# Second product of both squared-ReLU MLPs by Strassen's algorithm in a two-layer trunk

## The chip, the cores and the metric

One core of a Trainium2 chip. Its engines are TensorE (PE, matrix products out of SBUF into PSUM), VectorE (DVE), ScalarE (ACT), GpSimd (POOL) and SyncE (SP, which starts the DMA transfers). Each has its own list of instructions and executes it in that order; semaphores make one wait for another. The time is the device time of one launch in microseconds (us), and lower is better.

## The reference, cut to what matters

A hidden state h of 1040 tokens (16 learned ones ahead of 1024) by 1024 features goes through two layers. Layer 0 has a mixer of recurrent channels, layer 1 a chunked state-space mixer (SSD); each is followed by the same kind of MLP, and both with a residual.

```
SEQ, N_META, D_MODEL, D_FF, DEPTH = 1024, 16, 1024, 4 * 1024, 2

def sq_relu_mlp(h, w_up, w_down):
    return jnp.square(jax.nn.relu(h @ w_up)) @ w_down

h = jnp.concatenate([meta, x], axis=1)
for layer in range(DEPTH):
    hn = rmsnorm(h, norm_mix[layer])
    mix = even_mixer(hn, ...) if layer % 2 == 0 else ssd_mixer(hn, ...)
    h = h + mix
    h = h + sq_relu_mlp(rmsnorm(h, norm_mlp[layer]), mlp_w_up[layer], mlp_w_down[layer])
h = rmsnorm(h, norm_final)
return h[:, N_META:]
```

The first product of an MLP makes 4096 hidden features from 1024, the second makes 1024 from 4096. Everything is float32. After the mixer of layer 1 the 16 learned tokens are not needed any more, so its MLP works on 1024 tokens.

## The kernel before

The state lies in SBUF with features on the 128 partitions: 8 feature tiles (KT) by tokens. Tokens come in three tiles: 400, 384 and 256 in the MLP of layer 0 (TT), 384, 384 and 256 in that of layer 1 (TL). PE takes float32 data here in a rounded form (fp32r), so each operand is split into a rounded part "hi" and the rest "lo", and one product of float32 matrices is three matmuls: hi by hi, hi by lo and lo by hi (mm3, L160 to L164). A matmul multiplies a 128 by 128 block of weights with as many columns as there are tokens in the tile. Weights come from HBM in halves of 512 columns (wraw); ACT rounds them (L156) and DVE, for some of them POOL, subtracts (L157).

An MLP has 32 tiles of 128 hidden features, taken in 16 blocks of two. do_up makes the hidden tiles of a block: for each of three token tiles and both feature tiles one up_unit of 24 matmuls (8 feature tiles by three) into one PSUM tile. DVE then applies the relu and the factor of the norm (L356), POOL squares (L357), ACT rounds (L358) and DVE subtracts (L359). do_down is the second product: for each token tile and each of the 8 output tiles n, 6 matmuls (two hidden tiles by three) into one PSUM tile, which DVE adds to the state (L400: "h<-h,mm"). So a block has 6 x 24 = 144 matmuls in its first product and 3 x 8 x 6 = 144 in its second.

The main loop emits the first product of block b + 1 ahead of the second product of block b. The last pass does the second products of the last two blocks together, 12 matmuls for each PSUM tile, and beside each added output tile it squares and sums for the next norm and splits the state where the next stage wants it so (L263, L286 to L288; after layer 1 the final norm). The weights of the first product have two buffers of each of two tags (w, u), those of the second two of tag d. PSUM has 8 banks of 512 float32 columns: four buffers "mm" for products and four "sm" for sums.

The order in each engine's list is made when the program is built, by a scheduler that starts from the order in which the code emits and moves an instruction forward where it reckons that its operands and buffers are ready; `shifted` gives some functions an earlier or later place. No table of numbers sets it by hand.

## Time and profile before

| | |
|---|---|
| median of 3 runs | 2831.54 us (2829.19 to 2836.15) |
| the profiled execution | 2833.13 us, its span in the trace 2831.4 us, granted TensorE clock 0.986 on the average |
| MLP of layer 0 | its first evictions (L400) at 435.7 us, its last pass from about 1070 to 1118 us |
| MLP of layer 1 | from about 2100 us, last pass from about 2771 to 2819 us, last eviction at 2819.5 us |
| instructions on PE and DVE | 17625 matmuls, 4043 DVE instructions |

The profile is one execution, taken by the hardware profiler. A busy PE means that a matmul is in flight; matmuls overlap, so how fast they follow each other is read from the distance between their starts in the timeline. The granted clock is TensorE's, 1.00 being the full 2.4 GHz. "idle before" is time in which an engine waited for the releaser named. Names after the arrow are the tiles that an instruction reads, the ones ahead of it what it writes.

### The profile page before, as it was taken

To read this page: it belongs to the slowest core of one execution; us is meant where nothing else is said; L and a number is where in the kernel's file an instruction comes from. 1 tells how busy PE (TensorE), PEld (TensorE's weight loads), DVE (VectorE), ACT (ScalarE), POOL (GpSimd) and SP (SyncE) were. 2 spreads that over 40 slices of the span, in tenths; PEclk is the share of its full clock that TensorE was granted. 3 is DMA by queue.
4 is the path that set the end of the run, shared out by engine and by line. 5 is a ranking of instruction groups with operands and counts; after the bars stand their busy time and mean duration, and the time that the engine had idled before them with its cause. 6 is when DMAs were issued, how large, how long until landed. Compare 5 with 4: busy or idle time off the path is not lost.

```text
span 2831.4 us, 45178 instructions
## 1 busy us (share of the span) xinstructions
PE 2740.4 (97%) x17625; PEld 2676.8 (95%) x17625; DVE 1832.7 (65%) x4043; ACT 927.5 (33%) x1953; POOL 626.5 (22%) x765
## 2 busy tenths in 40 slices
PE   7998999999999999999999999999899999999998
PEld 7887999999999999899999999998889999999998
DVE  9887465555555556776876767778884555555555
ACT  4556241112111113444443444435551112121113
POOL 2212121101010113243332333324441111010112
PEclk9989999999999999999999999999999999999999
DMA  4432320101111110121221212213321101011111
GB/s 163 110 77 57 120 68 31 60 31 60 38 53 51 40 60 18 51 79 53 73 74 44 80 51 70 77 50 110 95 68 37 60 31 60 30 60 42 49 49 60
DMA packets 117909, 176.37 MB, mean 62 GB/s; under 512 B 13376, under 2 KB 47936, under 8 KB 117568
## 3 DMA queue, kind: packets, MB, share of 16 engines
q1 hardware_dynamic: 117408, 173.34, 19.8%
q8 instruction: 138, 2.26, 0.3%
q14 instruction: 75, 0.61, 0.1%
q10 hardware_dynamic: 288, 0.15, 0.0%
HBM read 158.34 MB, written 8.72 MB: 59 GB/s over the span
## 4 chain that ended last, share of the span: by engine, by line
PE 77%; DVE 15%; ACT 2%; issue 2%; DMA 2%; POOL 1%; SPq 0%; DVEq 0%; POOLq 0%; ACTq 0%
PE mm L163 24%; PE mm L162 24%; PE mm L164 23%; DVE xbc L1094 3%; DMA csb<-csd 1%; PE mm L1204 1%; DVE lo L288 1%; PE sm L1208 1%; PE mm L1201 1%; PE sm L1167 1%; PE sm L250 1%; DVE wlo L157 1%; DVE zs L1230 1%; PE sm L233 0%; DVE xbc L1096 0%
## 5 line engine op out<-in xcount | busy, mean ns | idle before, releaser
L162 PE MATMUL mm<-hi,whi 128*128 128x256 f32 (+2 forms) x2400 | 787.5, 328 | 16.1 <-ACT whi L156 8.5
L164 PE MATMUL mm<-hi,wlo 128*128 128x256 f32 (+2 forms) x2400 | 772.2, 322 | 3.1 <-POOL wlo L157 3.1
L163 PE MATMUL mm<-lo,whi 128*128 128x256 f32 (+2 forms) x2400 | 773.9, 323 | 1.2 <-POOL lo L280 0.6
L400 DVE TENSOR_TENSOR h<-h,mm 128x384 f32<-128x384 f32 (+1 forms) x720 | 368.8, 512 | 301.6 <-PE mm L164 299.6
L162 PEld LDWEIGHTS mm<-hi,whi 128*128 128x128 f32 x2400 | 456.6, 190 | 22.0 <-ACT whi L156 9.7
L164 PEld LDWEIGHTS mm<-hi,wlo 128*128 128x128 f32 x2400 | 456.3, 190 | 4.2 <-POOL wlo L157 3.8
L163 PE MATMUL mm<-hl,dhi 128*128 128x384 f32 (+2 forms) x1440 | 459.5, 319 | 0.0
L164 PE MATMUL mm<-hh,dlo 128*128 128x384 f32 (+2 forms) x1440 | 459.4, 319 | 0.0
L163 PEld LDWEIGHTS mm<-lo,whi 128*128 128x128 f32 x2400 | 455.5, 190 | 4.2 <-POOL lo L280 0.9
L162 PE MATMUL mm<-hh,dhi 128*128 128x384 f32 (+2 forms) x1440 | 459.3, 319 | 0.1
L357 POOL TENSOR_TENSOR s<-s 128x384 f32<-128x384 f32 (+2 forms) x192 | 162.7, 848 | 1187.8 <-DVE s L356 1086.3
L156 ACT CAST dhi<-wraw 128x512 fp32r<-128x512 f32 x120 | 68.9, 620 | 651.0 <-PE mm L163 574.8
L162 PEld LDWEIGHTS mm<-hh,dhi 128*128 128x128 f32 x1440 | 271.9, 189 | 0.3 <-DVE h L400 0.3
L164 PEld LDWEIGHTS mm<-hh,dlo 128*128 128x128 f32 x1440 | 272.0, 189 | 0.0
L163 PEld LDWEIGHTS mm<-hl,dhi 128*128 128x128 f32 x1440 | 271.9, 189 | 0.0
L163 PE MATMUL mm<-lo,uhi 128*128 128x384 f32 (+2 forms) x768 | 245.3, 319 | 0.0
L164 PE MATMUL mm<-hi,ulo 128*128 128x384 f32 (+2 forms) x768 | 245.0, 319 | 0.0
L162 PE MATMUL mm<-hi,uhi 128*128 128x384 f32 (+2 forms) x768 | 244.9, 319 | 0.0
L1094 DVE SCALAR_TENSOR_TENSOR xbc<-s,cols,xbc 128x400 f32<-128x400 f32 (+2 forms) x288 | 205.4, 713 | 25.6 <-ACT xbc L1092 23.5
L358 ACT CAST hh<-s 128x384 fp32r<-128x384 f32 (+2 forms) x192 | 92.3, 481 | 393.1 <-POOL s L357 393.1
L359 DVE TENSOR_TENSOR hl<-s,hh 128x384 fp32r<-128x384 f32 (+2 forms) x192 | 99.5, 518 | 147.5 <-ACT hh L358 145.2
L356 DVE SCALAR_TENSOR_TENSOR s<-mm,rb 128x384 f32<-128x384 f32 (+2 forms) x192 | 98.9, 515 | 146.4 <-PE mm L164 143.2
(367 smaller groups left out, 4400.0 us busy)
## 6 DMA issues: line engine op xcount, KB each, us to landing
wraw<-in_mlp_up SPq DMA_DIRECT2D x128, 256.0 KB
wraw<-in_mlp_down SPq DMA_DIRECT2D x128, 256.0 KB
wraw<-in_ssd_in SPq DMA_DIRECT2D x120, 256.0 KB
csb<-csd SPq DMA_DIRECT2D x64, 256.0 KB
sa<-ecd SPq DMA_DIRECT2D x128, 64.0 KB
wraw<-in_ssd_out SPq DMA_DIRECT2D x32, 256.0 KB
wraw<-in_ev_in SPq DMA_DIRECT2D x24, 256.0 KB
wraw<-in_ev_out SPq DMA_DIRECT2D x18, 256.0 KB
```

The lines of the kernel that those rows point to most:

```text
L156: nc.scalar.copy(hi[:, s], raw)
L157: e.tensor_tensor(out=lo[:, s], in0=raw, in1=hi[:, s].bitcast(F32), op=ALU.subtract)
L162: nc.tensor.matmul(pt, lhsT=whi, rhs=xhi, start=first, stop=False)
L163: nc.tensor.matmul(pt, lhsT=whi, rhs=xlo, start=False, stop=False)
L164: nc.tensor.matmul(pt, lhsT=wlo, rhs=xhi, start=False, stop=last)
L250: self.nc.tensor.matmul(st[:, o:o + l], lhsT=y[:l, i:i + 1].broadcast_to([l, P]), rhs=self.ident[:l, :l], start=True, stop=True)
L356: nc.vector.scalar_tensor_tensor(out=r, in0=pt[:, :w], scalar=0.0, in1=rbs[i], op0=ALU.max, op1=ALU.mult)
L357: nc.gpsimd.tensor_tensor(out=sq, in0=r, in1=r, op=ALU.mult)
L358: nc.scalar.copy(hh, sq)
L359: nc.vector.tensor_tensor(out=hl, in0=sq, in1=hh.bitcast(F32), op=ALU.subtract)
L400: nc.vector.tensor_tensor(out=hs, in0=hs, in1=pt[:, :w], op=ALU.add)
L1094: v.scalar_tensor_tensor(out=ot, in0=raw[:, k:k + w], scalar=cw(k), in1=ot, op0=ALU.mult, op1=ALU.add)
```

## The change

In 14 of the 16 blocks of each MLP the second product is done by the Strassen-Winograd scheme. The block's weights (two hidden tiles by 1024 outputs) and its hidden squares (two hidden tiles by all tokens) are each cut in four quarters: hidden tile 0 or 1; lower or upper half of the outputs (4 tiles each); lower or upper half of the tokens, 520 each in layer 0 and 512 each in layer 1. Seven products of a combination of weight quarters with a combination of hidden quarters take the place of eight. Four of the seven go straight into a quarter of the state ("2", "5", "3", "4"), and three into sums in SBUF ("1", "6", "7": acc, 4 output tiles by half of the tokens each) that are kept over all 14 blocks and spread over the state once, by 14 additions of two output tiles by half of the tokens (combine). For that, one quarter of the state is subtracted from another at the start. The 15th block is done in eight quarter products ("c11" to "c22"), while combine runs; the last pass now holds one block, four output tiles at a time.

The combinations are made by POOL into two buffers, ca for weights and cb for the hidden layer. Each operand of a product, a piece, is rounded by ACT and its low part subtracted by POOL for weights (sw) and by DVE for the hidden layer (sx); hi and lo lie together in one of six buffers "pc". Weights of the second product come in four quarters of 512 columns (draw, six buffers). The pieces of a product are emitted two products ahead of it. Hidden squares are no more split when they are made: ACT squares into one tile, and POOL's square and DVE's subtraction (L357, L359) are gone. A product has one piece of weights (128 by 512) and one of the hidden layer (128 by 520 or 512) and four output tiles: in layer 0 four PSUM pairs of two banks, each one output tile with 2 x 260 tokens, 6 matmuls a pair and 24 a product; in layer 1 two pairs, each two output tiles with 512 tokens, again 6 matmuls a pair, 12 a product. An eviction takes a whole pair (L502 of the changed kernel). In the MLP's blocks PSUM holds three such pairs (pd) and two single banks (ps) for everything else, and for the last pass it goes back to four and four.

The first product's units now go hidden tile by hidden tile with the three token tiles inside, and one unit is emitted after each product.

```diff
+        self.H = cp.tile([P, KT, NTOK], F32, name="h")
+        self.h = [self.H[:, :, o:o + w] for o, w in TT]
...
+    def psum(self, wide):
+        if self.pstack:
+            self.pstack.close()
+        self.pstack = st = ExitStack()
+        self.npsum += 1
+        pool = lambda name, bufs: st.enter_context(self.tc.tile_pool(name=f"{name}{self.npsum}", bufs=bufs, space=PSUM))
+        self.pd = pool("pd", 3) if wide else None
+        self.ps = pool("ps", 2 if wide else 4)
+        self.pss = None if wide else pool("pss", 4)
...
+        if tag == "pc":
+            hi, lo = (self.piece(pool)[:, :1024] for _ in range(2))
...
-    def up_unit(self, tls, ws, i, f, pool, tag, rbs):
-        r, sq = self.scr("s0", w), self.scr("s1", w)
-        hh, hl = (pool.tile([P, w], F32R, name=f"{q}{tag}{i}{f}", bufs=1) for q in ("hh", "hl"))
+        r = self.scr("s0", w)
         nc.vector.scalar_tensor_tensor(out=r, in0=pt[:, :w], scalar=0.0, in1=rbs[i], op0=ALU.max, op1=ALU.mult)
-        nc.gpsimd.tensor_tensor(out=sq, in0=r, in1=r, op=ALU.mult)
-        nc.scalar.copy(hh, sq)
-        nc.vector.tensor_tensor(out=hl, in0=sq, in1=hh.bitcast(F32), op=ALU.subtract)
+        nc.scalar.activation(out=dst[:, o - t0:o - t0 + w].bitcast(F32), in_=r, func=AF.Square)
         self.tick()
-        return hh, hl
+    def piece(self, mp):
+        return mp.tile([P, self.pcw], F32R, name="pc", bufs=6)
+    def split2(self, mp, x, e):
+        nc = self.nc
+        w = x.shape[-1]
+        t = self.piece(mp)
+        hi, lo = t[:, :w], t[:, w:2 * w]
+        nc.scalar.copy(hi, x)
+        e.tensor_tensor(out=lo, in0=x, in1=hi.bitcast(F32), op=ALU.subtract)
+        return hi, lo
...
+        NB = 16
+        t0, hw, subs = (0, 520, ((0, 260), (260, 260))) if layer == 0 else (META, 512, ((0, 512),))
+        halves = slice(t0, t0 + hw), slice(t0 + hw, t0 + 2 * hw)
+        rbs = {} if rbs is None else rbs
+        W, sq = dict(enumerate(ahead)), {}
+        if early:
+            sq[0] = [early[f] for f in range(2)]
+        def hidden(b):
+            if b not in sq:
+                q = ep if ep and b % 2 == 0 else mp
+                sq[b] = [q.tile([P, 2 * hw], F32R, name=f"sq{f}" if ep else f"sq{b % 2}{f}", bufs=1) for f in range(2)]
+            return sq[b]
...
+        def ups(b):
+            hid = hidden(b)
+            for f in range(2):
+                for i in range(3):
+                    if not (early and b == 0 and i == 0):
+                        self.up_unit(tls, [W[2 * b], W[2 * b + 1]], i, f, ep if ep and i == 0 else mp, hid[f], t0, rbs)
+                        yield
+                n = 2 * b + f + 2
+                if n < 32 and n not in W:
+                    W[n] = self.load_w(up[n])
...
+                    r = mp.tile([P, 512], F32, name="draw", bufs=6)
+                    nc.sync.dma_start(r, down[2 * b + f][:, q * 512:q * 512 + 512])
...
+        sw = lambda x: self.split2(mp, x, pool)
+        sx = lambda x: self.split2(mp, x, v)
+        def seven(b):
+            (w11, w12, w21, w22), (b11, b12, b21, b22) = quarters(b)
+            ca = mp.tile([P, 512], F32, name="ca", bufs=1)
+            cb = mp.tile([P, hw], F32, name="cb", bufs=1)
+            def comb(a0, a1, aop, x0, x1):
+                pool.tensor_tensor(out=ca, in0=a0, in1=a1, op=aop)
+                if x0 is not None:
+                    pool.tensor_tensor(out=cb, in0=x0, in1=x1, op=ALU.subtract)
+            yield "1", [(sw(w11), sx(b11))]
+            yield "2", [(sw(w12), sx(b21))]
+            comb(w21, w22, ALU.add, b12, b11)
+            yield "5", [(sw(ca), sx(cb))]
+            comb(ca, w11, ALU.subtract, b22, cb)
+            yield "6", [(sw(ca), sx(cb))]
+            comb(w12, ca, ALU.subtract, None, None)
+            yield "3", [(sw(ca), sx(b22))]
+            pool.tensor_tensor(out=cb, in0=b21, in1=cb, op=ALU.subtract)
+            yield "4", [(sw(w22), sx(cb))]
+            comb(w11, w21, ALU.subtract, b22, b12)
+            yield "7", [(sw(ca), sx(cb))]
...
+        def eight(b):
+            (w11, w12, w21, w22), (b11, b12, b21, b22) = quarters(b)
+            a = sw(w11), sw(w12)
+            x = sx(b11), sx(b21)
+            yield "c11", list(zip(a, x))
...
+        acc = {k: mp.tile([P, 4, hw], F32, name=f"acc{k}", bufs=1) for k in "167"}
+        H = lambda r, c: self.H[:, 4 * r:4 * r + 4, halves[c]]
+        dest = {"1": acc["1"], "6": acc["6"], "7": acc["7"], "2": H(0, 0), "5": H(1, 1), "3": H(0, 1), "4": H(1, 0),
+                "c11": H(0, 0), "c12": H(0, 1), "c21": H(1, 0), "c22": H(1, 1)}
+        step = 2 if len(subs) == 1 else 1
+        def product(key, pairs, copy):
+            for m in range(0, 4, step):
+                pt = self.pd.tile([P, 1024], F32, name="pd")
+                p2 = pt.rearrange("p (a b) -> p a b", a=2)
+                for q in range(2):
+                    n, (o, w) = (m + q, subs[0]) if step == 2 else (m, subs[q])
+                    ns = slice(n * P, n * P + P)
+                    for j, ((ah, al), (xh, xl)) in enumerate(pairs):
+                        self.mm3(p2[:, q, :w], ah[:, ns], al[:, ns], xh[:, o:o + w], xl[:, o:o + w], j == 0, j == len(pairs) - 1)
+                d = dest[key][:, m:m + step]
+                if step == 1:
+                    d = d.rearrange("p a (s w) -> p (a s) w", s=2)
+                src = p2[:, :, :subs[0][1]]
+                if copy and key in acc:
+                    nc.scalar.copy(d, src)
+                else:
+                    v.tensor_tensor(out=d, in0=d, in1=src, op=ALU.add)
+        def combine():
+            add = lambda a, b, n: v.tensor_tensor(out=a[:, n:n + 2], in0=a[:, n:n + 2], in1=b[:, n:n + 2], op=ALU.add)
+            a1, a6, a7 = (acc[k] for k in "167")
+            for x, y in (H(0, 0), a1), (a6, a1), (H(0, 1), H(1, 1)), (a7, a6), (H(0, 1), a6), (H(1, 0), a7), (H(1, 1), a7):
+                for n in (0, 2):
+                    add(x, y, n)
+                yield
...
+        self.psum(True)
+        for n in range(0, 4, 2):
+            d = H(0, 1)[:, n:n + 2]
+            v.tensor_tensor(out=d, in0=d, in1=H(1, 1)[:, n:n + 2], op=ALU.subtract)
+        items = (it for b in range(NB - 1) for it in (seven(b) if b < NB - 2 else eight(b)))
+        queue = deque()
+        fetch = lambda: queue.append(next(items))
...
-        for b in range(NB - 2):
-            nh = do_up(b + 1)
-            wd = down_w(b)
-            for i in range(3):
-                do_down([(wd, hid)], i)
-            hid = nh
+        for b in range(NB - 2):
+            u = ups(b + 1)
+            for j in range(7):
+                if j == 3:
+                    rows(b + 1)
+                last = b == NB - 3 and j > 4
+                if not last:
+                    fetch()
+                elif j == 6:
+                    fetch()
+                product(*queue.popleft(), b == 0)
+                next(u, None)
...
+        u = ups(NB - 1)
+        com = combine()
+        for j in range(4):
+            if j < 3:
+                fetch()
             else:
+                wd = [self.load_w(down[2 * NB - 2], mp, "pc")]
+            product(*queue.popleft(), False)
+            for _ in range(2):
+                next(u, None)
+                next(com, None)
...
+        wd.append(self.load_w(down[2 * NB - 1], mp, "pc"))
+        self.psum(False)
...
+        for i, (o, w) in enumerate(tls):
+            off = o - TT[i][0]
+            hs = lambda n: self.h[i][:, n, off:off + w]
+            pts = {}
+            for n in range(KT):
+                for f, m in ((f, m) for f in range(2) for m in (range(n, n + 4) if n % 4 == 0 else ())):
+                    if f == 0:
+                        pts[m] = self.mm()
+                    ms = slice(m * P, (m + 1) * P)
+                    h, q = (z[:, o - t0:o - t0 + w] for z in hid[f])
+                    self.mm3(pts[m][:, :w], wd[f][0][:, ms], wd[f][1][:, ms], h, q, f == 0, f == 1)
+                v.tensor_tensor(out=hs(n), in0=hs(n), in1=pts[n][:, :w], op=ALU.add)
```

Line numbers after the change are those of the changed kernel: its mm3 has L179 to L181, the weights' subtraction L174, a hidden piece's subtraction L386, the relu eviction L372, the product's eviction L502, the last pass's eviction L583.

PE in layer 0, where a block's last unit of the first product ends (mm_5972, third token tile) and the second product begins (mm_6025), before:

```order
L162 MATMUL mm_5972<-hi2_80,whi_5797 128x256
L163 MATMUL mm_5972<-lo2_83,whi_5797 128x256
L164 MATMUL mm_5972<-hi2_80,wlo_5798 128x256
L162 MATMUL mm_6025<-hh000_5404,dhi_6005 128x400
L163 MATMUL mm_6025<-hl000_5405,dhi_6005 128x400
L164 MATMUL mm_6025<-hh000_5404,dlo_6006 128x400
L162 MATMUL mm_6025<-hh001_5437,dhi_6015 128x400
```

After the change, PE at the joint of two blocks of layer 0: the last pair of product "7" (pd_5496) and the first of product "1" of the next block (pd_5522); each pd is a PSUM pair:

```order
L179 MATMUL pd_5496<-pc_5335,pc_5332 128x260
L180 MATMUL pd_5496<-pc_5335,pc_5332 128x260
L181 MATMUL pd_5496<-pc_5335,pc_5332 128x260
L179 MATMUL pd_5522<-pc_5403,pc_5400 128x260
L180 MATMUL pd_5522<-pc_5403,pc_5400 128x260
L181 MATMUL pd_5522<-pc_5403,pc_5400 128x260
L179 MATMUL pd_5522<-pc_5403,pc_5400 128x260
```

The end of the third pair of the same product and its fourth pair (pd_5538, pd_5546), a little further in the same list:

```order
L180 MATMUL pd_5538<-pc_5403,pc_5400 128x260
L181 MATMUL pd_5538<-pc_5403,pc_5400 128x260
L179 MATMUL mm_5556<-hi0_76,whi_5292 128x400
L180 MATMUL mm_5556<-lo0_79,whi_5292 128x400
L181 MATMUL mm_5556<-hi0_76,wlo_5293 128x400
L179 MATMUL mm_5556<-hi0_76,whi_5292 128x400
L180 MATMUL mm_5556<-lo0_79,whi_5292 128x400
L179 MATMUL pd_5546<-pc_5403,pc_5400 128x260
L180 MATMUL pd_5546<-pc_5403,pc_5400 128x260
L181 MATMUL pd_5546<-pc_5403,pc_5400 128x260
```

Before, 144 matmuls of the first product are followed by 144 of the second, each PSUM tile a single bank. After, no unit of the first product stands between products "7" and "1", so eight pairs follow each other, broken only by five matmuls of the next unit (mm_5556) ahead of the eighth pair.

DVE in one block of the middle of layer 0, before. h_75, h_76, h_77 are the state's three token tiles, s a relu'd tile, dlo and wlo low parts of weights:

```order
L356 SCALAR_TENSOR_TENSOR s_7254<-mm,rb_4024 128x256
L359 TENSOR_TENSOR hl_7257<-s_7255,hh_7256 128x256
L356 SCALAR_TENSOR_TENSOR s_7287<-mm,rb_4024 128x256
L400 TENSOR_TENSOR h_75<-h_75,mm 128x400
L359 TENSOR_TENSOR hl_7290<-s_7288,hh_7289 128x256
L400 TENSOR_TENSOR h_75<-h_75,mm 128x400 x7
L400 TENSOR_TENSOR h_76<-h_76,mm 128x384 x8
L400 TENSOR_TENSOR h_77<-h_77,mm 128x256 x8
L157 TENSOR_TENSOR dlo<-wraw,dhi 128x512 x4
```

DVE at the joint of two blocks of layer 0 after the change. acc_3842 is the sum "7", acc_3840 the sum "1", pc<-cb the low part of a hidden piece, wlo that of a weight of the first product:

```order
L372 SCALAR_TENSOR_TENSOR s_7833<-mm,rb_3979 128x256
L174 TENSOR_TENSOR wlo<-wraw,whi 128x512
L502 TENSOR_TENSOR acc_3842<-acc_3842,pd 128x520 x4
L174 TENSOR_TENSOR wlo<-wraw,whi 128x512
L386 TENSOR_TENSOR pc<-cb,pc 128x520
L502 TENSOR_TENSOR acc_3840<-acc_3840,pd 128x520 x4
L386 TENSOR_TENSOR pc<-cb,pc 128x520
L372 SCALAR_TENSOR_TENSOR s_7951<-mm,rb_3898 128x400
L502 TENSOR_TENSOR h<-h,pd 128x520 x4
L386 TENSOR_TENSOR pc<-sq_7451,pc 128x520
L372 SCALAR_TENSOR_TENSOR s_8019<-mm,rb_3947 128x384
L502 TENSOR_TENSOR h<-h,pd 128x520 x4
```

Before, the 24 evictions of a block stand in one row, with the four weight subtractions of the next block behind them. After, they come in rows of four, one for each product, and between them stand the relu evictions, the weight subtractions and the subtractions of pieces for products to come.

## Rows read from the trace of the kernel before

**Rows 1.** The page's first part: engine, busy us (share of the span) xinstructions.

```profile
span 2831.4 us, 45178 instructions
...
PE 2740.4 (97%) x17625; PEld 2676.8 (95%) x17625; DVE 1832.7 (65%) x4043; ACT 927.5 (33%) x1953; POOL 626.5 (22%) x765
```

**Rows 2.** Windows in the MLPs: start:end, us, busy by engine (instructions), PEclk, DMA, GB/s.

```profile
700.00:800.00 100.00, 100.00 (x648) 100.00 (x647) 53.13 (x96) 16.68 (x31) 11.87 (x15) 1.00 0.14 43
1070.00:1118.00 48.00, 47.93 (x307) 47.38 (x306) 29.70 (x69) 17.51 (x37) 13.07 (x13) 1.00 0.05 15
1110.00:1140.00 30.00, 27.46 (x165) 25.93 (x164) 29.90 (x77) 16.05 (x37) 12.84 (x19) 0.94 0.03 10
2500.00:2600.00 100.00, 100.00 (x634) 100.00 (x633) 53.97 (x99) 15.51 (x29) 10.96 (x13) 1.00 0.13 43
2771.00:2819.00 48.00, 47.75 (x309) 46.78 (x307) 26.29 (x68) 25.12 (x48) 15.03 (x15) 1.00 0.16 58
```

**Rows 3.** Timeline of PE, 700 to 730: start us, us, engine, line, operation, count.

```profile
701.09 0.28 PE L162 MATMUL mm<-hi,whi 128*128 128x256 f32 x1
...
706.55 0.34 PE L162 MATMUL mm<-hh,dhi 128*128 128x400 f32 x1
...
715.25 0.34 PE L162 MATMUL mm<-hh,dhi 128*128 128x384 f32 x1
...
723.57 0.28 PE L162 MATMUL mm<-hh,dhi 128*128 128x256 f32 x1
...
729.32 0.34 PE L162 MATMUL mm<-hi,uhi 128*128 128x400 f32 x1
```

**Rows 4.** Timeline of PE, 88 to 92, narrow matmuls of layer 0's mixer.

```profile
88.81 0.39 PE L683 MATMUL mm<-s5ug,s5M 128*128 128x130 f32 x2
...
91.27 0.39 PE L685 MATMUL mm<-s5w,s5G 128*128 128x130 f32 x2
```

**Rows 5.** Groups by line and shape: busy us, mean ns; idle before, releasers.

```profile
L400 DVE TENSOR_TENSOR h<-h,mm 128x256 f32<-128x256 f32 x240 | 100.9, 421 | 63.9 <-PE mm L164 63.8
...
L157 DVE TENSOR_TENSOR dlo<-wraw,dhi 128x512 fp32r<-128x512 f32 x120 | 77.6, 686 | 33.8 <-ACT dhi L156 33.7
...
L156 ACT CAST dhi<-wraw 128x512 fp32r<-128x512 f32 x120 | 68.9, 620 | 651.0 <-PE mm L163 574.8 <-DMA wraw<-in_mlp_down 76.2
L400 DVE TENSOR_TENSOR h<-h,mm 128x400 f32<-128x400 f32 x120 | 68.5, 571 | 61.6 <-PE mm L164 60.3
...
L356 DVE SCALAR_TENSOR_TENSOR s<-mm,rb 128x256 f32<-128x256 f32 x64 | 27.2, 424 | 24.3 <-PE mm L164 22.5 <-ACT rb L353 0.7
```

**Rows 6.** Timeline of DVE near the end, two evictions in a row.

```profile
2815.86 0.77 DVE L400 TENSOR_TENSOR h<-h,mm 128x256 f32<-128x256 f32 x2
```

**Rows 7.** Tile whi: duration ns min/median/max, first and last start us, forms.

```profile
L157 DVE TENSOR_TENSOR wlo<-wraw,whi x168: 667/685/1386, 8.4 to 2757.9; 128x512 fp32r<-128x512 f32 x168
L157 POOL TENSOR_TENSOR wlo<-wraw,whi x62: 1261/1302/1909, 15.0 to 2033.8; 128x512 fp32r<-128x512 f32 x62
```

**Rows 8.** Timeline of POOL and DVE in the last pass of layer 0.

```profile
1110.83 1.21 POOL L280 TENSOR_TENSOR lo<-s,hi 128x400 fp32r<-128x400 f32 x1 [1.30 <-ACT hi L278]
1111.07 1.25 DVE L288 SCALAR_TENSOR_TENSOR lo<-h,cols,hi 128x256 fp32r<-128x256 f32 x1
...
1116.77 0.47 DVE L288 SCALAR_TENSOR_TENSOR lo<-h,cols,hi 128x256 fp32r<-128x256 f32 x1
```

**Rows 9.** Line L400: duration ns min/median/max, first and last start us, forms.

```profile
L400 DVE TENSOR_TENSOR h<-h,mm x720: 404/554/574, 435.7 to 2819.5; 128x384 f32<-128x384 f32 x90, 128x256 f32<-128x256 f32 x60, 128x400 f32<-128x400 f32 x30
```

**Rows 10.** Timeline of PE, the last matmul of the last pass of layer 1.

```profile
2818.77 0.28 PE L164 MATMUL mm<-hh,wlo 128*128 128x256 f32 x1
```

120 lines of the change are left out of this document (66 added, 54 removed).

## The prediction

> **What bounds the kernel now.** I read the page's first part first [rows 1]: PE is busy for 2740.4 us of a span of 2831.4, VectorE (DVE) for 1832.7, ACT and POOL far less. A busy PE could still be a slow one, so the windows inside the two MLPs come next [rows 2]: in 700 to 800 and in 2500 to 2600 PE is busy for all 100 us at a granted clock of 1.00, DVE for about 53, ACT for 16, POOL for 12. There only fewer or shorter matmuls help. The timeline of PE shows what one costs [rows 3]: starts follow each other without a gap, so the distance between starts, not the 0.28 or 0.34 us that each is long, is its price. In one block of the second product 48 matmuls of 400 columns take 715.25 - 706.55 = 8.70 us, 0.1813 each; 48 of 384 take 8.32, 0.1733 each; 48 of 256 take 5.75, 0.1198 each; together 22.77 us. In the first product just before, 48 of 256 take 706.55 - 701.09 = 5.46, 0.1138 each: one width at two prices, 5% apart. Very narrow ones don't get cheaper in proportion: between 88.81 and 91.27 lie 22 of 130 columns, 0.112 each [rows 4].
>
> **The change: PE.** Outside the MLPs every engine's order is the same, row for row. In each layer 14 of 16 blocks now take seven products of a quarter's size where there were eight.
> Layer 0 before: 16 x 22.77 = 364.3 us. Now 14 x 7 x 24 = 2352 matmuls of 260 columns, 192 more in the block that keeps eight, and the last block as before (22.8). Scaled by width from the two prices of 256, one of 260 costs 0.1156 to 0.1217; I take 0.1187, the middle. 2544 x 0.1187 = 302.0, and with 22.8 it is 324.8: 39.5 less (31.9 to 47.4).
> Layer 1 before (384, 384, 256): 16 x 48 x (2 x 0.1733 + 0.1198) = 358.2 us. Now 14 x 7 x 12 + 96 = 1272 of 512 columns, and 22.4. No row has 512; in proportion the rows of 256 give 0.2276 and 0.2396, those of 384 and 400 give 0.2311 and 0.2321. I take 0.2315, by the widest rows: 294.5 + 22.4 = 316.9, 41.3 less (31.0 to 46.3).
> Sum: 81 us less PE work (63 to 94).
> The Trainium skill, TensorE: Matmul & The Clock Gate, Back-to-back issue gap, gives N / 2.4 + 2.5 ns for a gap: 110.8 ns at 260 columns, 215.8 at 512. By it the sum would be 59.6 + 61.7 = 121. Rows 3 disagree: 0.1138 and 0.1198 where it says 0.109, 0.1813 where it says 0.169.
>
> **The change: DVE and POOL in a block.** An eviction costs 0.421 us for 256 columns and 0.571 for 400 [rows 5], 1.04 ns a column: 0.70 for 520, 1.22 for 1024. In a row they overlap a little, two of 256 take 0.77 [rows 6]; in a burst I use 0.66 for 520. A subtraction of 512 columns with both sources in SBUF takes 0.69 on DVE [rows 5] and 1.30 on POOL [rows 7], an ACT cast 0.62 [rows 5]. Per block of layer 0:
> DVE has 28 evictions (19.6), 7 subtractions for pieces of the hidden layer (4.8), 4 for the up weights (2.8), 6 relu evictions (about 3.1): 30.3 us. PE has 168 x 0.1187 = 19.9, and 22.8 for the first product: 42.7. POOL has 7 subtractions and 8 combinations, 15 x 1.30 = 19.5. ACT has 18 casts and 6 squares, about 14. On the average all three hide behind PE.
> DVE and POOL get in each other's way: at 1110.83 a POOL subtraction runs for 1.21, and a DVE instruction that starts at 1111.07 takes 1.25 instead of 0.47 [rows 8]; an up-weight subtraction has a median of 685 ns and a maximum of 1386 [rows 7]. Evictions from PSUM never exceed 574 ns [rows 9]. With POOL busy 46% of the time and half an instruction left, 0.65, each of the 11 SBUF subtractions waits 0.3 us: 3.3 a block, DVE 33.6 of 42.7.
> This is where a rule speaks against the change: the Trainium skill, SBUF - State Buffer, Who interferes with whom, calls the port pair that the two share an exclusive lock, so that moving work to POOL isn't free for DVE. The trace agrees for SBUF sources (0.47 to 1.25); without such a lock the 7 us below would be about 1.
> What can be late is the burst. Product 7 of a block and product 1 of the next stand back to back on PE, as the rows of the order show: eight PSUM pairs of 6 x 0.1187 = 0.71 us in three buffers, so the eighth needs the fifth evicted. DVE by then has a relu 0.42 [rows 5], a weight 0.69, four evictions 2.64, a weight 0.69, a piece 0.69 and one eviction 0.66, and three waits of 0.3: 5.8 to 6.7 us. PE is there after 7 x 0.71 = 5.0, but the order puts five matmuls of the next up unit first, 0.9 more. I take a wait of 0.4, and 0.1 at product 4, which also follows a weight: 0.5 a block, 7 us in layer 0 (0 if POOL is never in the way; 2.0 a block, 28, with the three waits at 0.70 = 1386 - 685 ns each). In layer 1 a pair lasts 6 x 0.2315 = 1.39 us and the burst has four: the fourth needs the first evicted at 0.42 + 1.38 + 1.22 = 3.0, with waits 3.6, and comes at 4.2. I take 2 us for the layer (0 to 8).
>
> **The change: the edges.** Start of each layer: two subtractions of 1040 columns, the switch of the PSUM pools and the first pieces, 1 us each (0 to 3).
> The block that keeps eight, with the recombination: DVE has 14 additions of 1040 columns (0.69 + 528 x 1.04 ns = 1.24 each, 17.3), 16 evictions 10.6, 8 weight and 4 piece subtractions 8.3, relu and last hidden pieces 6.2: 42 us, with waits about 46, beside 4 products and 6 up units, 45.6 on PE. It is full: 4 us in layer 0, 3 in layer 1 (2 to 14 together).
> The last pass: before, it holds two blocks, 45.5 us of PE; now one, 22.8, with the same squares, sums and norm beside it. In 1070 to 1118 DVE was busy for 29.7 us, in 2771 to 2819 DVE for 26.3 and ACT for 25.1 [rows 2]: all exceed 22.8. In layer 0 DVE was full behind it anyway (29.90 of 30 in 1110 to 1140, PE 27.46 [rows 2]), so I count half of the 7 us of excess as new: 4 (1 to 9). In layer 1 ACT and DVE take turns, so the pass ends some 28 us after its start: 5 (2 to 9). The tail from the last matmul at 2818.77 [rows 10] stays as it is.
> Sum of losses: 2 + 7 + 2 + 7 + 4 + 5 = 27 us.
> The profiled execution took 2833.13 us, 1.7 more than its span. 2833.1 - 81 + 27 = 2779; the median of the three runs is 1.6 lower, so the forecast is 2778.
>
> **The rivals.**
> Hidden all through: DVE and POOL cost nothing in blocks and recombination, the last passes lose 11 in all. For it: the averages above. 2831.5 - 81 + 11 = 2762.
> Bursts: each block of layer 0 loses 2.0 us instead of 0.5, POOL being in the way when it matters. For it: the maximum in rows 7; against it: the median there, which is undisturbed. 2778 + 21 = 2799.
> The gap as the page has it: matmuls of 260 and 512 columns, in their new places, start every 0.111 and 0.216 us: 121 us less instead of 81, 2738. Against it: no row is as fast for its width.
> Slower than before: the pieces don't come in time. Each product needs a chain of POOL combination, ACT cast and POOL or DVE subtraction, with one buffer for each combined operand and six for pieces; the DVE subtraction stands behind the evictions of the product before, and until it has read its operand POOL may not overwrite it. If PE waits for that in each of 2 x 98 products, it decides from (81 - 18) / 196 = 0.32 us a product, 18 being the losses at the edges. At 0.5 us it is 98: 2831.5 - 81 + 18 + 98 = 2867. Against it: pieces are prepared two products ahead, some 13 us, and the chain is 1.3 + 1.3 + 0.6 + 1.3 = 4.5.
>
> **How the numbers follow.** Forecast 0.42 (its own range 2764 to 2793), hidden 0.18, bursts 0.22, the page's gap 0.06, slower 0.12. The range 2750 to 2815 holds the first three with the bounds of 260 and 512 columns and leaves out the last two, 0.18. What lies within 0.3% (8.5 us) can't be told from no change. Faster: the first four less 0.01, 0.87; same 0.02; slower 0.11.
>
> **What would show it.** Right: matmuls into the new PSUM pairs start 0.116 to 0.122 us apart at 260 columns and 0.228 to 0.240 at 512, 168 and 84 a block; PE busy for over 98 of 100 us in the middle of both layers; DVE at about 75 of 100 in layer 0; PE's waits on DVE at the second of two adjoining products and in the last passes. Wrong: PE waiting for ACT's casts or POOL's low pieces in the middle of a layer (the slower rival), evictions that grow when POOL is busy, or matmuls of 260 columns over 0.125.

## The result and the profile after

The changed kernel takes 2794.67 us (median of 4 runs, 2792.95 to 2798.76) against 2831.95 before: a ratio of 0.9869, 95% interval 0.9852 to 0.9886. That is 37 us less. The forecast was 54 us less, 2778, in a range of 2750 to 2815. The profiled execution took 2793.77 us with a span of 2792.0, 39.4 less than before. Where the two traces part is read from the last matmul of each stage:

| stretch | before | after | change | forecast |
|---|---|---|---|---|
| start to the last matmul of layer 0's MLP | 1118.0 | 1109.4 | -8.6 | -23.5 |
| from there to the last matmul of the SSD mixer | 980.1 | 983.7 | +3.6 | 0 |
| from there to the last matmul of layer 1's MLP | 720.7 | 679.9 | -40.8 | -30.3 |
| from there to the end | 12.6 | 19.1 | +6.4 | 0 |

Layer 1 gave more than was forecast, layer 0 a third of it, and the end costs what no term of the sum had.

The page's first part of the changed kernel, which answers to [rows 1]: span and busy time.

```profile
span 2792.0 us, 44635 instructions
...
PE 2677.5 (96%) x17121; PEld 2554.3 (91%) x17121; DVE 2118.9 (76%) x3901; ACT 1104.8 (40%) x2275; POOL 1077.8 (39%) x1005
```

The windows in the changed kernel, with the columns of [rows 2]; the third is its last pass of layer 1, the fourth what follows:

```profile
700.00:800.00 100.00, 97.72 (x698) 96.44 (x697) 78.43 (x103) 29.63 (x55) 48.68 (x35) 1.00 0.15 49
...
2500.00:2600.00 100.00, 100.00 (x553) 92.36 (x552) 74.52 (x75) 31.18 (x58) 50.79 (x37) 1.00 0.18 56
2744.00:2773.00 29.00, 26.79 (x162) 26.14 (x162) 20.91 (x55) 18.87 (x41) 10.58 (x10) 0.94 0.15 56
2773.00:2792.00 19.00, 4.60 (x20) 4.01 (x19) 10.69 (x37) 3.81 (x11) 3.84 (x4) 0.57 0.39 138
```

PE is still full in layer 1 and no longer in layer 0, though DVE is at 75 to 78 of 100 us in both, against 53 before. The prices of the matmuls come from the timeline of PE (start us, us), the first ones of a product and the first of the unit behind it. Layer 0, 24 of 260 columns:

```profile
730.53 0.28 PE L179 MATMUL pd<-pc 128*128 128x260 f32 x1
...
733.42 0.34 PE L179 MATMUL mm<-hi,whi 128*128 128x384 f32 x1
...
743.27 0.28 PE L179 MATMUL pd<-pc 128*128 128x260 f32 x1
...
746.66 0.34 PE L179 MATMUL mm<-hi,whi 128*128 128x400 f32 x1
```

Layer 1, 12 of 512:

```profile
2508.83 0.39 PE L179 MATMUL pd<-pc 128*128 128x512 f32 x1
...
2511.55 0.33 PE L179 MATMUL mm<-hi,whi 128*128 128x384 f32 x1
```

The first product shown takes 2.89 us, 0.1204 a matmul (others of the layer 2.86, 0.1192), where 0.1187 was forecast, and layer 1's 2.72, 0.2267, where it was 0.2315. The second product shown, "6", takes 3.39 us for the same 24 matmuls: 0.5 us of it is a wait. All 13 blocks from 440 to 1020 have one such product, 7.2 us of wait together. The list of PE's waits in 440 to 1030 (engine, line, waited for: us in total, times, longest) has nothing but DVE's evictions in it:

```profile
PE pd L179 <- DVE acc L502: 12.0, 25, 0.7
```

No cast of ACT and no piece of POOL is waited for. In product "6" it is a weight subtraction on DVE that comes late. It starts 0.69 us behind a combination of POOL and takes 1.17 us instead of 0.69, and the evictions stand behind it (POOL, DVE and PE there):

```profile
743.32 1.32 POOL L451 TENSOR_TENSOR cb<-sq,sq 128x520 f32<-128x520 f32 x1 [0.64 <-DVE pc L386]
...
744.01 1.17 DVE L174 TENSOR_TENSOR wlo<-wraw,whi 128x512 fp32r<-128x512 f32 x1
745.10 2.50 DVE L502 TENSOR_TENSOR acc<-acc,pd 128x520 f32<-128x520 f32 x4
...
745.84 0.39 PE L179 MATMUL pd<-pc 128*128 128x260 f32 x1 [0.27 <-DVE acc L502]
```

The larger wait is at the joint of two blocks. The timelines of DVE, POOL, ACT and PE there (what stands in brackets is idle time before and its releaser):

```profile
763.98 0.42 DVE L372 SCALAR_TENSOR_TENSOR s<-mm,rb 128x256 f32<-128x256 f32 x1 [0.23 <-PE mm L181]
764.51 0.69 DVE L174 TENSOR_TENSOR wlo<-wraw,whi 128x512 fp32r<-128x512 f32 x1
765.12 2.50 DVE L502 TENSOR_TENSOR acc<-acc,pd 128x520 f32<-128x520 f32 x4
767.55 0.68 DVE L174 TENSOR_TENSOR wlo<-wraw,whi 128x512 fp32r<-128x512 f32 x1
768.15 1.79 DVE L386 TENSOR_TENSOR pc<-cb,pc 128x520 fp32r<-128x520 f32 x1
769.86 1.29 DVE L502 TENSOR_TENSOR acc<-acc,pd 128x520 f32<-128x520 f32 x2
...
767.64 1.74 POOL L386 TENSOR_TENSOR pc<-ca,pc 128x512 fp32r<-128x512 f32 x1 [4.45 <-ACT pc L385]
...
766.94 0.62 ACT L385 CAST pc<-ca 128x512 fp32r<-128x512 f32 x1 [1.62 <-PE pd L181]
767.47 0.62 ACT L385 CAST pc<-cb 128x520 fp32r<-128x520 f32 x1
...
769.56 0.34 PE L180 MATMUL mm<-lo,whi 128*128 128x400 f32 x1
770.60 0.39 PE L179 MATMUL pd<-pc 128*128 128x260 f32 x1 [0.69 <-DVE acc L502]
```

ACT rounds the weight piece first and the hidden piece behind it, so POOL starts its subtraction at 767.64, DVE comes to its own at 768.15, and that takes 1.79 us instead of 0.69. (POOL's takes 1.74 instead of 1.30: it starts 0.09 us behind DVE's weight subtraction of 767.55.) The fifth eviction of the burst starts only at 769.86, and the eighth pair stands 1.04 us behind the matmul before it where 0.18 is usual: 0.86 us of wait, at 12 joints.

The last pass of layer 1, timeline of PE: last matmul of the last product, first of the pass, and the last one of all, which answers to [rows 10].

```profile
2741.63 0.39 PE L181 MATMUL pd<-pc 128*128 128x512 f32 x1
...
2744.05 0.41 PE L179 MATMUL mm<-acc,pc 128*128 128x384 f32 x1 [2.04 <-DVE h L502]
...
2768.95 0.39 PE L179 MATMUL mm<-acc,pc 128*128 128x256 f32 x1 [1.74 <-DVE h L583]
...
2772.95 0.28 PE L181 MATMUL mm<-acc,pc 128*128 128x256 f32 x1
```

The pass starts 2.2 us late (2.42 us between two starts where 0.23 is usual), since the switch of the PSUM pools waits for the last evictions, and from its first start to its last it takes 28.9 us for 22.4 us of matmuls. The pass of before, with twice the matmuls, takes 48.5 (2770.24 to 2818.77) for 44.8, so 3.7 of these 6.5 us were there before. The chain of waits shows what is left over behind the pass, the final norm of the second token tile, in the changed kernel and in the one before:

```profile
2780.67 1.85 DVE h L337 x4
...
2813.75 1.86 DVE h L320 x4
```

Before, these four stand five us ahead of the last matmul; here they start 7.7 us after it.

### The profile page after: what moved, and what is told of

Read it like the earlier page. It is cut to its first block, busy times and chain, and to the rows that moved or that the text cites. A ratio compares the mean times of both kernels' runs of the same rounds, so it can differ in the third digit from the quotient of the medians.

```text
span 2792.0 us, 44635 instructions
## 1 busy us (share of the span) xinstructions
PE 2677.5 (96%) x17121; PEld 2554.3 (91%) x17121; DVE 2118.9 (76%) x3901; ACT 1104.8 (40%) x2275; POOL 1077.8 (39%) x1005
## 4 chain that ended last, share of the span: by engine, by line
PE 72%; DVE 19%; ACT 3%; issue 3%; POOL 2%; DMA 2%; SPq 0%; DVEq 0%; ACTq 0%; POOLq 0%
PE mm L179 16%; PE mm L180 16%; PE mm L181 16%; PE pd L179 6%; PE pd L181 6%; PE pd L180 6%; DVE xbc L1261 3%; DVE wlo L174 2%; DVE acc L502 2%; PE mm L1371 1%; ACT whi L173 1%; PE sm L1375 1%; DVE pc L386 1%; PE mm L1368 1%; PE sm L267 1%
## 5 line engine op out<-in xcount | busy, mean ns | idle before, releaser
L179 PE MATMUL mm<-hi,whi 128*128 128x384 f32 (+2 forms) x3120 | 1020.3, 327 | 19.7 <-ACT whi L173 9.8
L180 PE MATMUL mm<-lo,whi 128*128 128x384 f32 (+2 forms) x3120 | 1007.9, 323 | 0.8 <-DVE lo L940 0.4
L181 PE MATMUL mm<-hi,wlo 128*128 128x384 f32 (+2 forms) x3120 | 1005.7, 322 | 2.7 <-POOL wlo L174 2.7
L179 PEld LDWEIGHTS mm<-hi,whi 128*128 128x128 f32 x3120 | 593.8, 190 | 30.6 <-ACT whi L173 11.1
L181 PEld LDWEIGHTS mm<-hi,wlo 128*128 128x128 f32 x3120 | 595.1, 191 | 3.8 <-POOL wlo L174 3.5
L179 PE MATMUL pd<-pc 128*128 128x260 f32 (+1 forms) x1272 | 408.0, 321 | 14.4 <-DVE acc L502 12.0
L180 PE MATMUL pd<-pc 128*128 128x260 f32 (+1 forms) x1272 | 404.2, 318 | 0.0
L181 PE MATMUL pd<-pc 128*128 128x260 f32 (+1 forms) x1272 | 404.1, 318 | 0.0
L502 DVE TENSOR_TENSOR h<-h,pd 128x520 f32<-128x520 f32 (+1 forms) x360 | 312.7, 871 | 68.0 <-PE pd L181 53.4
L386 POOL TENSOR_TENSOR pc<-draw,pc 128x512 fp32r<-128x512 f32 x96 | 131.7, 1375 | 419.9 <-ACT pc L385 409.6
L179 PEld LDWEIGHTS pd<-pc 128*128 128x128 f32 x1272 | 238.8, 188 | 34.9 <-DVE acc L502 18.7
L181 PEld LDWEIGHTS pd<-pc 128*128 128x128 f32 x1272 | 239.3, 188 | 16.6
L180 PEld LDWEIGHTS pd<-pc 128*128 128x128 f32 x1272 | 239.2, 188 | 13.1
L386 POOL TENSOR_TENSOR pc<-ca,pc 128x512 fp32r<-128x512 f32 x112 | 156.0, 1393 | 235.2 <-ACT pc L385 231.9
L173 ACT CAST whi<-wraw 128x512 fp32r<-128x512 f32 x286 | 167.2, 618 | 155.6 <-PE mm L180 137.6
L372 DVE SCALAR_TENSOR_TENSOR s<-mm,rb 128x384 f32<-128x384 f32 (+2 forms) x192 | 98.8, 515 | 170.4 <-PE mm L181 156.3
L502 DVE TENSOR_TENSOR acc<-acc,pd 128x520 f32<-128x520 f32 (+1 forms) x234 | 189.1, 859 | 4.0 <-PE pd L181 4.0
L174 DVE TENSOR_TENSOR wlo<-wraw,whi 128x512 fp32r<-128x512 f32 x224 | 167.0, 764 | 17.1 <-ACT whi L173 10.3
L386 DVE TENSOR_TENSOR pc<-cb,pc 128x520 fp32r<-128x520 f32 (+1 forms) x112 | 149.3, 1333 | 38.7 <-ACT pc L385 38.7
```

Source lines behind the costliest of these rows:

```text
L173: nc.scalar.copy(hi[:, s], raw)
L174: e.tensor_tensor(out=lo[:, s], in0=raw, in1=hi[:, s].bitcast(F32), op=ALU.subtract)
L179: nc.tensor.matmul(pt, lhsT=whi, rhs=xhi, start=first, stop=False)
L180: nc.tensor.matmul(pt, lhsT=whi, rhs=xlo, start=False, stop=False)
L181: nc.tensor.matmul(pt, lhsT=wlo, rhs=xhi, start=False, stop=last)
L372: nc.vector.scalar_tensor_tensor(out=r, in0=pt[:, :w], scalar=0.0, in1=rbs[i], op0=ALU.max, op1=ALU.mult)
```

## The experiments

All ratios are to the kernel before, with 95% intervals; the changed kernel's own is 0.9869. The kernel before was run again beside each set of experiments, with medians from 2829.86 to 2833.64 us, so a difference of 4 us between two rows of the table may be one between sets.

| kernel | us | ratio |
|---|---|---|
| weights' low pieces left out (hilo) | 2780.58 | 0.9816 (0.9801 to 0.9831) |
| weight of the second tile later (latew) | 2790.84 | 0.9844 (0.9829 to 0.9860) |
| last pass of two blocks (last2) | 2779.09 | 0.9810 (0.9793 to 0.9827) |
| only layer 1 changed (l1only) | 2796.64 | 0.9873 (0.9858 to 0.9889) |
| weight pieces subtracted on DVE (lodve) | 2771.41 | 0.9794 (0.9778 to 0.9810) |
| first product's weights on POOL (wpool) | 2777.65 | 0.9814 (0.9799 to 0.9828) |
| last2, later PSUM switch, latew (best1) | 2773.38 | 0.9802 (0.9788 to 0.9817) |
| last2, later PSUM switch, wpool (best2) | 2760.78 | 0.9755 (0.9740 to 0.9769) |
| hidden piece cast first (xfirst) | 2775.10 | 0.9800 (0.9786 to 0.9814) |
| last2, later PSUM switch, lodve (best3) | 2751.62 | 0.9720 (0.9706 to 0.9734) |

**Which layer gave the gain.** Layer 0's MLP as before, layer 1's by the change:

```diff
-                    self.mlp(0, TT, mp, ahead, "nmix1" if "c" in stages else None)
+                    self.mlp0(0, TT, mp, ahead, "nmix1" if "c" in stages else None)
```

> Layer 0 does its MLP as before the change, layer 1 by the changed one. By the stretches of the two traces layer 0 gains 8.6 us up to its last product and loses 3.3 in the handover to the next mixer, so the theory that nearly all of the gain is layer 1's expects 2798 to 2802. The forecast's own split, 23 us from layer 0 and 30 from layer 1, expects 2805 or, scaled to the measured gain of 37, about 2811.

It takes 2796.64, 1.4 us below the range of the first theory and 8 or more below the second; with layer 0 changed as well it is 2794.67, and the intervals overlap. What layer 0 gave is too small to be told from nothing in these times; the rest was layer 1's.

**POOL's subtraction left out.** The weight piece's rounded part stands for its low part too, so POOL's subtraction is gone and PE's work is the same:

```diff
         nc.scalar.copy(hi, x)
+        if e is nc.gpsimd:
+            return hi, hi
         e.tensor_tensor(out=lo, in0=x, in1=hi.bitcast(F32), op=ALU.subtract)
```

> The low part of each weight piece of the seven products is left out and its rounded part multiplied in its place, so PE, ACT and DVE have the same instructions and POOL loses its 7 subtractions a block. In the trace of the changed kernel PE waits 0.86 us at each of 12 joints of layer 0 (1.04 between two starts where 0.18 is usual), and the DVE subtraction of a hidden piece, which stands there ahead of the fifth eviction, takes 1.71 us. Theory A (POOL in the way of DVE): that subtraction falls to about 0.7 to 1.0 us, the wait to 0 to 0.2, and the time by 9 to 14 us from 2794.7, to 2781 to 2786. Theory B (the queue on DVE is too long whatever POOL does): the waits stay at 0.7 or more and the time within 4 us of 2794.7.

The time fell as theory A had it (2780.58, 0.4 us below its range), the place was another. Product "6" lost its wait of 0.5, but the joints kept theirs: 12 gaps of 1.02 to 1.07. The line of the hidden pieces' subtraction in this kernel (duration ns min/median/max):

```profile
L388 DVE TENSOR_TENSOR pc<-cb,pc x112: 684/1306/1812, 416.9 to 2670.9; 128x520 fp32r<-128x520 f32 x56, 128x512 fp32r<-128x512 f32 x56
L388 DVE TENSOR_TENSOR pc<-sq,pc x92: 682/700/1390, 399.6 to 2697.9; 128x520 fp32r<-128x520 f32 x46, 128x512 fp32r<-128x512 f32 x46
```

Pieces cut straight from the hidden squares fell to 700 ns (median); in the changed kernel they have a median of 1365. Those made from a combination did not, because POOL, free of its subtraction, now starts its next combination at that moment: at the joint one of 1.74 us from 500.37, and DVE's piece from 500.89, again 1.79. So it isn't POOL's subtraction as such: a combination that has started does the same.

**What stands in DVE's queue.** The second tile's weight is loaded one unit later:

```diff
-                n = 2 * b + f + 2
-                if n < 32 and n not in W:
-                    W[n] = self.load_w(up[n])
+                    n = 2 * b + 1 if f == 0 and i == 0 else 2 * b + 2 if f == 0 and i == 2 else 32
+                    if n < 32 and n not in W:
+                        W[n] = self.load_w(up[n])
```

> The weight of the second hidden tile of a block is loaded and split after the block's first unit and no longer at the joint of two blocks. DVE then has one weight subtraction and one piece fewer ahead of the fifth eviction of the burst (0.6 + 1.7 us), and PE no longer has five matmuls of the next unit there. Theory B (what is queued on DVE between the evictions makes the eighth pair late): the wait at the joint falls from 0.86 to under 0.2 us in 12 or 13 joints, 9 to 11 us less, about 2785. Theory C (eight pairs in three buffers are too many for DVE in any case, since four evictions take 2.5 us and four pairs of matmuls 2.9): the wait stays at 0.5 or more, 2791 or more. Theory A expects some of it too, since the slowed subtraction no longer stands ahead of the fifth eviction.

Theory B was right of the burst and wrong of the sum. The burst now runs 48 matmuls in 5.76 us, 0.120 each, without a wait. The weight subtraction lands beside the next product, runs into POOL's combination there and takes 1.79 us, and PE waits 0.53 us there for an eviction of that product; product "6" keeps its wait. A block takes 44.1 us instead of 44.4: 3.8 us in all.

**POOL or DVE for the weight pieces.**

```diff
-        sw = lambda x: self.split2(mp, x, pool)
+        sw = lambda x: self.split2(mp, x, v)
```

> The low part of each weight piece is subtracted on DVE instead of POOL, nothing else changes: 7 subtractions of 512 columns a block move. In the trace of the changed kernel a hidden piece's subtraction takes 1.37 to 1.79 us whenever POOL's subtraction of the same product's weight piece, released by ACT a moment before, runs beside it, against 0.69 alone. Theory A (the two engines shut each other out of SBUF, so an operation costs DVE the same wherever it runs): DVE's hidden pieces fall to 0.7 to 1.0 us, the two pieces of a product take DVE about as long together as the one took, and the time stays within 5 us of 2794.7. Rival (POOL's work runs beside DVE's at little cost): DVE gets 4.8 us a block more and each burst waits some 0.7 us longer: 2804 or more.

Both theories missed. It gained 23 us, where theory A had at most 5: no wait is left on PE from 440 to 1030, and layer 0's MLP ends at 1091.5 instead of 1109.4. DVE has 4.8 us a block more to do and isn't busier: 76.0 of 100 us in 700 to 800 against 78.4. Its joint, DVE and POOL:

```profile
760.33 0.68 DVE L174 TENSOR_TENSOR wlo<-wraw,whi 128x512 fp32r<-128x512 f32 x1
760.93 0.68 DVE L386 TENSOR_TENSOR pc<-ca,pc 128x512 fp32r<-128x512 f32 x1
761.53 0.69 DVE L386 TENSOR_TENSOR pc<-cb,pc 128x520 fp32r<-128x520 f32 x1
762.14 2.55 DVE L502 TENSOR_TENSOR acc<-acc,pd 128x520 f32<-128x520 f32 x4
...
761.69 1.70 POOL L449 TENSOR_TENSOR ca<-ca,draw 128x512 f32<-128x512 f32 x1 [17.04 <-DVE pc L386]
```

Two subtractions one after the other take DVE 1.21 us here, one beside POOL 1.79 there. And here POOL starts 0.16 us after DVE's second one, and DVE's still takes 0.69. Who is first seemed to decide; the next experiment changes only that.

**The same work, the other order.** ACT casts the hidden piece first:

```diff
-            yield "1", [(sw(w11), sx(b11))]
+            yield "1", [xw(w11, b11)]
...
+        def xw(a, x):
+            px = sx(x)
+            return sw(a), px
```

> ACT casts the hidden piece of a product ahead of the weight piece and no longer behind it; the lists of DVE and POOL are the same, and so is the work. Moving POOL's subtractions to DVE had taken 23 us, more than either theory said: the hidden pieces took 0.69 us even where POOL's combination ran beside them for half a us. Theory G (whichever of the two engines starts first keeps the other out until it is done): where DVE is free when its cast is done it now starts first, its piece takes 0.7 instead of 1.37, and POOL's subtraction grows to about 1.9; at the joint of two blocks DVE is still busy with a weight when POOL starts, so the wait of 0.86 there stays; the other waits, about 0.5 a block, go: 2784 to 2790. Rival H (both slow each other down as long as they overlap, whoever is first): pieces stay at 1.3 or more on the average, 2792 to 2797.

Theory G holds in who keeps out whom, and missed where that pays: it gave 20 us instead of the 5 to 11 expected. The joint, whose wait was to stay, has lost it:

```profile
501.66 0.69 DVE L174 TENSOR_TENSOR wlo<-wraw,whi 128x512 fp32r<-128x512 f32 x1
502.26 0.69 DVE L386 TENSOR_TENSOR pc<-cb,pc 128x520 fp32r<-128x520 f32 x1
...
502.34 1.76 POOL L386 TENSOR_TENSOR pc<-ca,pc 128x512 fp32r<-128x512 f32 x1 [4.42 <-ACT pc L385]
```

In both kernels the piece starts 0.60 us behind the weight subtraction's start, so its earlier cast gains it no time on DVE, only the place ahead of POOL. The waits of 0.5 in product "6", which were to go, are all 13 still there (the list of PE's waits in 440 to 1000 counts their idle part):

```profile
PE pd L179 <- DVE acc L506: 2.9, 13, 0.2
```

What stands in the way there is the weight subtraction behind POOL's combination, and the order of the casts doesn't change that pair (1.15 us at 737.45, behind a combination of 736.72). Of the 20 us, 13.7 are layer 0's, whose MLP ends at 1095.7; 4.9 are the MLP of layer 1 and what follows it. The lines of the pieces in this kernel, DVE's and POOL's:

```profile
L386 DVE TENSOR_TENSOR pc<-cb,pc x112: 682/694/1700, 417.4 to 2666.3; 128x520 fp32r<-128x520 f32 x56, 128x512 fp32r<-128x512 f32 x56
L386 POOL TENSOR_TENSOR pc<-ca,pc x112: 1267/1376/1812, 418.1 to 2665.6; 128x512 fp32r<-128x512 f32 x112
L386 POOL TENSOR_TENSOR pc<-draw,pc x96: 1276/1670/2354, 400.6 to 2704.4; 128x512 fp32r<-128x512 f32 x96
```

In 480 to 1000, 72 of DVE's 84 pieces start ahead of the POOL instruction that they overlap, with a median of 700 ns; in the changed kernel all 82 start behind one, with a median of 1368. How they wait can be read from the ends: all 82 end 0.55 to 0.56 us after POOL's instruction does, however long before it started. With the casts swapped, the 84 POOL instructions that start behind a subtraction of DVE end 1.15 to 1.22 us after it.

**No weight subtraction on DVE.**

```diff
-                    W[n] = self.load_w(up[n])
+                    W[n] = self.load_w(up[n], lo_pool=True)
```

> The four weight subtractions a block of the first product move from DVE to POOL. Moving the weight of the second tile by one unit had emptied the burst at two blocks' joint but set the fourth pair of the next product waiting for 0.53 us, where a weight subtraction of 1.79 then stood beside POOL's work. Theory B (whatever stands on DVE between two groups of evictions is what PE waits for): with no weight subtraction on DVE the waits of 0.86 and of about 0.5 a block go, 12 to 18 us of layer 0, 2778 to 2784. Rival (POOL, at 19.5 + 5.2 of 44 us by its own times, now lets pieces come late or only slows the remaining pieces on DVE): 2790 or more.

As theory B expected, 0.35 us below its range: layer 0's MLP ends at 1090.2, and from 440 to 1030 PE has one wait on DVE left, 1.2 us in the block that keeps eight, though the hidden pieces still take 1.28 and 1.37. So the wait at the joint goes either by a shorter queue or by a faster piece; each alone suffices. The one in product "6" goes with the weight subtraction.

**The last pass.** It gets two blocks again, each PSUM tile 12 matmuls, and the block in eight quarter products is gone:

```diff
-        items = (it for b in range(NB - 1) for it in (seven(b) if b < NB - 2 else eight(b)))
+        items = (it for b in range(NB - 2) for it in seven(b))
...
+                for f in range(4):
+                    h, q = (z[:, o - t0:o - t0 + w] for z in hid[f][1:])
+                    self.mm3(pts[n][:, :w], *wd[f](n), h, q, f == 0, f == 3)
```

> The block in eight quarter products is gone: the last pass holds two blocks again, 12 matmuls for each output tile, as before the change, and the recombination stands beside the last units of the first product. The count of matmuls on PE is the same within 1%. Theory E (a last pass of one block, 22.8 us of PE, is too short for the squares, sums and norm beside it, so that PE waits in it and the final norm is left over): in layer 1 the last pass loses its 9 us over 22.4, the stretch from the last product to the end falls from 19.0 to about 12.6, and layer 0's handover and last pass lose 4 to 8: 2770 to 2780. Rival F (DVE is as full in the new stretch, which takes 12 more subtractions and 8 weights beside 14 additions, some 28 us beside 22.8 on PE, and only moves the wait ahead of the last pass): within 6 us of 2794.7.

2779.09, inside theory E's range, but not all by its sum. The stretch behind the last matmul is 12.5 us again, 6.6 shorter, and layer 0's MLP with the handover is 5.7 us shorter. The pass in layer 1 has no wait over 0.6 us, yet the stretch up to its end is only 1.1 us shorter (678.8), since the 9 us were counted against the matmuls alone and the longer pass brings its own sums and small waits back. Of rival F only the switch of PSUM ahead of the last units remained, 2.1 us in layer 1. With that switch behind the last units (`self.psum(False)` moved below them) and one of the other edits each:

> The last pass of two blocks, PSUM switched back only after the last units of the first product (where the switch ahead of them cost PE 2.1 us in layer 1 and 1.1 in layer 0), and the weight of the second tile one unit later. If the three are independent: 2779.1 less 3.8 for the weight less 2 to 3 for the switch, 2772 to 2774. If the wait of the switch only moves to the start of the last pass: 2775 to 2777.

> The same last pass and PSUM switch, with the weight subtractions of the first product on POOL. By theory B, whose price for them is 12 to 18 us: 2759 to 2766. By the rival, that POOL's work is paid by DVE's pieces: 2773 or more.

> Last pass of two blocks, PSUM switched after the last units, and the weight pieces' subtractions on DVE. Last pass and switch were worth 17 us beside the weights on POOL (2777.7 to 2760.8). If what DVE got for the pieces is independent of that: 2771.4 - 17 = 2754 to 2757. If DVE, which has 12 hidden subtractions and the additions beside the last units, is the one that is late there: 2759 or more.

best1 came to 2773.38 and best2 to 2760.78, each where the sum of its parts had it; best3 to 2751.62, 2 us below. It beats both kernels: 0.9720 of the time before. Its page and two of its windows:

```profile
span 2749.9 us, 44674 instructions
...
PE 2660.8 (97%) x17121; PEld 2549.6 (93%) x17121; DVE 2088.7 (76%) x4081; ACT 1105.4 (40%) x2275; POOL 798.8 (29%) x801
```

```profile
700.00:800.00 100.00, 100.00 (x735) 99.98 (x735) 77.05 (x122) 31.21 (x57) 24.21 (x17) 1.00 0.14 43
...
2690.00:2737.00 47.00, 46.74 (x304) 45.98 (x303) 26.02 (x68) 24.85 (x48) 14.44 (x14) 1.00 0.16 56
```

PE is full in layer 0, and the last pass of layer 1 reads like that of before in [rows 2].

## Why the prediction came out as it did

**The matmuls** were right. Layer 0's 2544 at 0.1199 (the mean of the products without a wait) are 305.0 us instead of 302.0, layer 1's 1272 at 0.2267 are 288.4 instead of 294.5: 84 us less PE work, forecast 81. Layer 1's price lies 0.4% under the lower bound taken from [rows 3], so proportion to the width was a little too dear there. The rival of the page's gap would have had 0.111 and 0.216; it is out. In the Trainium skill (TensorE: Matmul & The Clock Gate, Back-to-back issue gap) its formula stands for a single matmul and not for a stream of them, which the prediction passed over. (Layer 1's part by it is 61.3 and not 61.7; the sum stays 121.)

**The burst** was named in the right place and mis-sized. The term "0.4 and 0.1: 0.5 a block, 7 us in layer 0" measured 0.86 at the joint and 0.5 to 0.6 at product "6": 7.2 us plus 12 x 0.86 = 10.3, 17.5 us. lodve confirms the size, since without these waits layer 0 ends 17.9 us earlier. The step that failed is "each of the 11 SBUF subtractions waits 0.3 us". It took POOL's instruction to be met at random. But both subtractions of a product are released by two casts of ACT that follow each other, POOL's first, so DVE met POOL early in its instruction each time: 1.37 in the median instead of 0.69, and 1.79 at the joint. There the piece alone waits 1.1 us and the two weight subtractions nothing, which is little more than the three waits of 0.3. By these the prediction's own sum has the eighth pair 6.7 - 5.9 = 0.8 late; it took 0.4, half way to no wait at all, and that half is the larger slip at the joint. The other wait was put at product "4", and 0.1; it is in "6", behind a weight subtraction slowed by a combination. In [rows 8] the pair of 1110.83 and 1111.07 is this very case, POOL first and DVE a moment later; I read its length and not its order. The rule of the Trainium skill (SBUF - State Buffer, Who interferes with whom) that the two hold their port pair exclusively is borne out, and with it that an eviction with one source in SBUF is spared. Of the evictions of 520 columns into a sum, those beside a POOL instruction take 682 ns in the median and those without one 685. Their line, which answers to [rows 9] (minimum, median, maximum):

```profile
L502 DVE TENSOR_TENSOR acc<-acc,pd x234: 680/686/1222, 457.9 to 2698.5; 128x520 f32<-128x520 f32 x78, 128x1024 f32<-128x1024 f32 x39
```

(1222 is the longest of 1024 columns.) So the bursts rival, POOL being in the way when it matters, had the mechanism; its 2.0 us a block and its 2799 were too dear, but nearer than the forecast's 0.5 and 2778: 1.4 and 2794.67 were measured.

**Layer 1's burst** was forecast at 2 us and is 0: PE never waits in 2115 to 2741, although its pieces are slowed likewise, 1.17 us and 1.28 in the mean. A pair lasts 1.36 us there.

**The edges.** The block that keeps eight was forecast at 7 us and shows one wait of 1.4 in layer 0 and none in layer 1: too dear. The last passes were about right. What counts is what they lose beyond the pass of before, which takes 48.5 us for 44.8 of matmuls in layer 1 and 48.6 for 45.5 in layer 0. In layer 1 the new one loses 6.5 - 3.7 = 2.8 inside, and 2.2 go to the PSUM switch ahead of it, which no term had: 5.0 where 5 was put. In layer 0 it is 2 inside and 1 at the switch, 3 where 4 was put. Of the 2.8 in layer 1, 1.5 are ten matmuls that start 0.32 us apart instead of 0.173 after the wait, TensorE at its lower level (granted clock 0.50 from 2745 to 2748, 0.94 over the window shown); lodve, with the same wait, had none of that and took 27.3 us for the pass. "The tail stays as it is" failed: +6.4, because the norm that stood beside 45 us of matmuls no longer fits beside 22; with the pass of two blocks in last2 it is 12.5 again.

The handover to the SSD mixer, put at nothing, is 3.6 longer. In the changed kernel's trace PE stands idle several times between 1109.4 and 1114.1, and from 1113.2 to 1120.0 its granted clock is 0.50: 18 matmuls of 400 columns start 0.33 us apart instead of 0.18, 2.7 us. In the trace of before the clock is 1.00 from 1110 to 1130. Among the profiled runs, one each, the stretch takes 975.2 to 983.3 us where layer 0 ends with a pass of two blocks and 980.8 to 985.7 where it ends with one; the overlap is large enough that only part of the 3.6 can be put down to the change.

**The sum by layer.** Layer 0: 36 us less work, less 17.5 of waits, 1.2 at the start, 1.4 at the last quarter products, 3 at the last pass and 2 because the first product's 256 columns became dearer (last section) is about 11; 8.6 was measured, and the rest is not accounted for. Layer 1: 47 less, 5 lost: 42, and 40.8 was measured. The direction and the range held, in part by luck: terms that were too dear (the block that keeps eight by 5.6 us, layer 1's burst by 2) made up for some of those that were too cheap (layer 0's waits by 10.5, the tail by 6.4, the handover by up to 3.6). The gain came from the layer in which I had put less of it.

**The other rivals.** Hidden all through was true of layer 1 and false of layer 0. The slower case, pieces that come too late, did not happen: nothing on PE waits for ACT or POOL in the blocks. It would have begun at 0.32 us a product.

## What to carry to other kernels

When two engines exclude each other, don't price the clash as a chance from their busy shares: look at who releases both, and which starts first. Give the start to the engine that others wait for, or put both operations on it; here swapping two casts was worth 20 us, of which 13.7 can be placed in layer 0, and moving 143 us of work (208 subtractions of 0.69) onto the busier engine 23. And before cutting the work that covers a tail (norm, sums, evictions), set the cover that is left against the work that it hid.
